# Weight part buffers at eight places of a 512-byte line, lower activations 32 bytes off the upper, in a fp32-split decoder trunk

## The chip, the core and the metric

The kernel runs on one core of one Trainium2 chip. The metric is the device time of one execution in microseconds (us); three runs of the kernel before have a median of 1153.88 us (1153.59 to 1154.02). Engines are called by the profile's names: PE (TensorE, matmuls), PEld (TensorE's weight loads), ACT (ScalarE), DVE (VectorE), POOL (GpSimd) and SP (SyncE, which here only issues DMAs).

## The reference

One decoder layer on 256 tokens of width 2048, float32 throughout:

```
h    = rms_norm(x, norm1_g)
proj = h @ w_in                       # q, k, v and forget logits of 8 heads; q, k, v of 8 more
y_a  = forgetting attention (causal softmax with cumulated log-sigmoid gates)
y_b  = mixture of three dilated windows with a relative position bias
x    = x + concat(rms_norm(y_a), rms_norm(y_b)) @ w_out
h    = rms_norm(x, norm2_g)
x    = x + square(relu(h @ w_mlp_in)) @ w_mlp_out      # 2048 -> 8192 -> 2048
out  = rms_norm(x, final_norm_g)
```

Head size is 128. Nearly all of the arithmetic is in the four weight products.

## The kernel before

**Three products for one.** A float32 operand is split into an upper part (`..._hi`, rounded to the type fp32r) and a lower part (`..._lo`, the rest), and a product is upper x upper, upper x lower and lower x upper, accumulated in PSUM. So each 128-deep slice of a weight product is three PE matmuls.

**Chunks and steps.** The weights are cut into chunks of 512 columns: twelve for q, v and k ("qkv"), eight for the output projection ("o"), and four rounds of four up chunks ("u") and four down chunks ("d"). A step is 256 rows of a chunk, two 128-deep slices. SP loads four slices by one 1 MB DMA into one of four `raw` buffers. `split` makes the parts of a step: ACT copies `raw` to `whi` with rounding (L168) and DVE subtracts to get `wlo` (L169), both 128 x 1024. There are four buffers for each (`LEAD + 1`), and `split` runs up to `LEAD` = 3 steps ahead of PE.

**Which operand lies still.** A matmul has a stationary operand, 128 x 128, brought in by a weight load of its own (PEld) while the matmul before it runs, and a moving operand that streams through. In qkv, o and d (`product`, L299 to L301) the activations are stationary and the weight part moves, 512 columns at a time. In u (`turned_product`, L313) 128 columns of a weight part are stationary and the activations `aT_hi`, `aT_lo` move, 256 columns at a time, in the order (`whi`,`aT_hi`), (`whi`,`aT_lo`), (`wlo`,`aT_hi`). The profile writes the moving operand or the stationary one first by its own rule; the shape in a matmul's row is that of the moving operand.

**Activations.** `aT_hi` and `aT_lo` hold the normed, transposed input of qkv, and later that of u. `big_hi` and `big_lo` hold the attention's output for o (named `yT`) and the squared-ReLU hidden for d (`hT`). In the last down chunk (`last_chunk`) the first four steps' weight parts are put into `aT_hi` and `aT_lo`, which are free by then, and the last four into the weight part buffers; its second half of tokens runs as two passes of 256 columns.

**Places.** Every tile has an address within its partition. In the table "place" is that address modulo 512 bytes, in the program as it was built. A 128-column float32 stationary operand is 512 bytes of a partition, and every slice that a matmul takes of these tiles starts a multiple of 512 bytes into its tile, so a tile's place is that of all its operands.

| tile | place before | place after |
|---|---|---|
| four `whi` | 160, all | 192, 320, 448, 64 |
| four `wlo` | 160, all | 256, 384, 0, 128 |
| `aT_hi` | 480 | 480 |
| `aT_lo` | 480 | 0 |
| `big_hi`, `big_lo` | 160 | 192 |
| `q`, `v` parts | 480 | 0 |
| `k` parts, `p` parts (probabilities) | 288 | 320 |
| four `raw` | 160, 288, 416, 32 | 192, 320, 448, 64 |

Before, all of these are 32 bytes past a multiple of 64; after, all but `aT_hi` are multiples of 64.

**Order.** The program's order is written out by hand (`manual_schedule`); attention work runs as `side` work between the weight products of the chunks. The causal mask for scores is `mcat`, three 128-column blocks (triangle, zeros, triangle) of the constant `pk`.

Of the kernel before, what the change touches and what calls it, by code (L numbers as in the profile page):

```python
# [11 lines left out]
F32 = mybir.dt.float32  # L12
F32R = mybir.dt.float32r
# [6 lines left out]
P = 128  # L20
D_MODEL = 2048
SEQ = 256
TB = SEQ // P
HD = 128
NH = 8
D_GRP = NH * HD
D_FF = 4 * D_MODEL
KT = D_MODEL // P
CW = 512
# [7 lines left out]
QSCALE = HD ** -0.5  # L37

LEAD = 3
WARM, WARM2 = 8, 1  # L40


def _constants():
    i = np.arange(P)
    upto = (i[:, None] <= i[None, :]).astype(np.float32)
    after = (i[:, None] > i[None, :]).astype(np.float32)
    tri = np.where(i[None, :] <= i[:, None], 0.0, NEG).astype(np.float32)
    head = (i[:, None] % 32 == np.arange(NH)[None, :]).astype(np.float32)
    pack = np.concatenate([after, -upto, tri, np.zeros((P, P), np.float32), tri, head], axis=1)

    dist = 255 - np.arange(RW)
    d = np.maximum(dist, 0)
    exact = N_BUCKETS // 2
    df = np.maximum(d.astype(np.float32), np.float32(1.0))
    large = exact + (
        np.log(df / np.float32(exact)) / np.float32(math.log(REL_MAX / exact)) * np.float32(N_BUCKETS - exact)
    ).astype(np.int32)
    bucket = np.where(d < exact, d, np.minimum(large, N_BUCKETS - 1))
    count = np.zeros(RW, np.int64)
    for window, dil in PATTERNS:  # L60
        count += (dist >= 0) & (dist % dil == 0) & (dist <= window)
    pick = np.zeros((N_BUCKETS + 1, RW), np.float32)
    pick[bucket, np.arange(RW)] = 1.0
    pick[N_BUCKETS] = np.where(count > 0, np.log(np.maximum(count, 1)), NEG)
    return np.ascontiguousarray(pack), pick
# [3 lines left out]
def kernel(  # L69
# [23 lines left out]
    one = ctx.enter_context(tc.tile_pool(name="one", bufs=1))  # L93
    two = ctx.enter_context(tc.tile_pool(name="two", bufs=2))
    wraw = ctx.enter_context(tc.tile_pool(name="wraw", bufs=4))
    wsplit = ctx.enter_context(tc.tile_pool(name="wsplit", bufs=LEAD + 1))
    psum = ctx.enter_context(tc.tile_pool(name="psum", bufs=2, space=PSUM))
    dram = ctx.enter_context(tc.tile_pool(name="dram", bufs=1, space=DRAM))
    ctx.enter_context(tc.manual_schedule())
# [30 lines left out]
    def load(i):  # L130
        if i >= len(steps) or steps[i][1] % 2 or (steps[i][0], steps[i][1] // 2) in raws:
            return
        ci, s = steps[i]
        _, _, w, r0, c0, cols, _ = chunks[ci]
        t = wraw.tile([P, 4, CW + NH], F32, name="raw")
        src = w[r0 + s * 256:r0 + s * 256 + 512, c0:c0 + cols].rearrange("(k p) c -> p k c", p=P)
        raws[ci, s // 2] = t
        if i == 0:
            return t, src
        n = 2 if i == 2 else 4  # L140
        for k in range(0, 4, n):
            nc.sync.dma_start(t[:, k:k + n, :cols], src[:, k:k + n])

    def split(i, j0=0, n=2):
        if i >= len(steps):
            return
        if j0:
            return split_rows(i, j0, n)
        ci, s = steps[i]
        t = raws[ci, s // 2][:, 2 * (s % 2):2 * (s % 2) + 2, :]  # L150
        if ci == len(chunks) - 1 and s < 4:
            hi, lo = (a[:, 4 * s:4 * s + 4, :].rearrange("p (k j) s -> p k (j s)", k=2) for a in (aT_hi, aT_lo))
        else:
            hi, lo = (wsplit.tile([P, 2, CW], F32R, name=n) for n in ("whi", "wlo"))
        if chunks[ci][5] > CW:
            f = wsplit.tile([P, 2, 2 * NH], F32R, name="wf")
            fh, fl = f[:, :, :NH], f[:, :, NH:]
            nc.gpsimd.tensor_copy(fh, t[:, :, CW:])
            nc.gpsimd.tensor_tensor(fl, t[:, :, CW:], fh.bitcast(F32), op=ALU.subtract)
            forget_w[i] = f  # L160
        splits[i] = (hi, lo)
        split_rows(i, j0, n)

    def split_rows(i, j, n):
        ci, s = steps[i]
        hi, lo = (a[:, j:j + n, :] for a in splits[i])
        t = raws[ci, s // 2][:, 2 * (s % 2) + j:2 * (s % 2) + j + n, :CW]
        nc.scalar.activation(hi, t, AF.Copy)  # L168
        nc.vector.tensor_tensor(lo, t, hi.bitcast(F32), op=ALU.subtract)  # L169
# [27 lines left out]
    fb = one.tile([P, NH], F32, name="fb")  # L197
    relx = one.tile([N_BUCKETS + 1, NH], F32, name="relx")
    nc.vector.memset(relx, 1.0)
    pk = one.tile([P, 5 * P + NH], F32, name="pk")  # L200
    pick_sb = two.tile([P, RW], F32, name="pr")[:N_BUCKETS + 1]

    def small_loads():
# [4 lines left out]
        nc.sync.dma_start(pk, pack)  # L208
        nc.sync.dma_start(pick_sb, pick)

    mcat = pk[:, 2 * P:5 * P]
    head = pk[:, 5 * P:]
    gcat = one.tile([P, TB, P], F32R, name="gcat")


# [11 lines left out]
        nc.tensor.transpose(p[:, :k1], grow[:k1], ident[:k1, :k1])  # L227
        nc.vector.tensor_copy(gT[:, k0:k1], p[:, k0:k1])

    aT_hi = one.tile([P, KT, SEQ], F32R, name="aT_hi")  # L230
    aT_lo = one.tile([P, KT, SEQ], F32R, name="aT_lo")

    def split_psum(hi, lo, src, scale=None):
# [105 lines left out]
    def at(i, f, *a):  # L339
        side.setdefault(i, []).append((f, a))  # L340
# [69 lines left out]
    relT = one.tile([P, NH, SEQ], F32, name="relT")  # L410
# [60 lines left out]
    def scores(g, h):  # L471

        half, kind = groups[g][3:]
        hd = half * 4 + h
        qh, ql = qkv[g, "q"]
        kh, kl = qkv[g, "k"]
        s = psum.tile([P, 512], F32, name="sc")
        terms = ((qh, kh), (qh, kl), (ql, kh))
        spans = ((0, 0, P), (1, P, 3 * P))
        for t, c0, c1 in spans:  # L480
            if kind == 0:
                nc.tensor.matmul(s[:, c0:c1], gate_s[:, t * P:(t + 1) * P], decay[hd][:, :c1 - c0],  # L482
                                 start=True, stop=False)
            for n, (q, k) in enumerate(terms):
                nc.tensor.matmul(  # L485
                    s[:, c0:c1], q[:, h, t * P:(t + 1) * P], k[:, h, :c1 - c0],
                    start=n == 0 and kind == 1, stop=n == 2,
                )
        decay.pop(hd, None)
        neg = two.tile([P, 3 * P], F32, name="neg")  # L490
        pr = two.tile([P, 3 * P], F32, name="pr")
        st = two.tile([P, 3, TB], F32, name="st")
        for t, c0, c1 in spans:
            add = mcat[:, c0:c1] if kind == 0 else relT[:, hd, SEQ - (c1 - c0):]
            nc.vector.tensor_tensor_reduce(  # L495
                neg[:, c0:c1], s[:, c0:c1], add, -1.0, BIG, ALU.add, ALU.min, st[:, 0, t:t + 1]
            )
        for t, c0, c1 in spans:
            nc.scalar.activation(  # L499
                pr[:, c0:c1], neg[:, c0:c1], AF.Exp, bias=st[:, 0, t:t + 1], scale=-1.0,  # L500
                accum_out=st[:, 1, t:t + 1],
            )
        nc.vector.reciprocal(st[:, 2, :], st[:, 1, :])
        for t, c0, c1 in spans:
            nc.vector.tensor_scalar(pr[:, c0:c1], pr[:, c0:c1], st[:, 2, t:t + 1], None, op0=ALU.mult)
        probs[g, h] = pr
# [134 lines left out]
    def last_chunk(done):  # L641

        ci = len(chunks) - 1
        what, key, _, _, _, _, kts = chunks[ci]
        i0 = len(steps) - kts // 2
        c0 = D_MODEL - CW
        for t, a, b, n in ((0, 0, CW, 3), (1, 0, CW // 2, 3), (1, CW // 2, CW, 4)):
            acc = psum.tile([P, CW], F32, name="acc", bufs=4)
            for kt in range(kts):
                if t == 0 and kt % 2 == 0:  # L650
                    split(done + 1 + kt // 2)
                product(acc[:, :b - a], operands(what, key), kt, t, splits[i0 + kt // 2], kt % 2, slice(a, b),
                        kt == 0, kt == kts - 1)
                if t == 0:
                    run_side(2 * i0 + kt)
            if b == CW:
                sum_before(t, n)
            add_down(acc, t, slice(c0 + a, c0 + b), n)
            if b == CW:
                finish(t, n, slice(c0 + a, c0 + b))  # L660
# [6 lines left out]
    for ci, (what, key, *_rest) in enumerate(chunks[:-1]):  # L667
# [8 lines left out]
        elif what in "qk":  # L676
# [4 lines left out]
            if what == "k":  # L681
                kind = groups[key][4]
                for h in range(4):
                    n = e + 6 + 4 * h
# [20 lines left out]

    idle_products(WARM)
    split(0, 0, 1)
    gains(0, 16)
    to_features(0, 0, 1)
    split(0, 1, 1)  # L710
    to_features(1, 0, 1)
    idle_products(WARM2)
# [13 lines left out]
    at(21, nc.vector.tensor_copy, gcat, pk[:, :2 * P].rearrange("p (t s) -> p t s", t=TB))  # L726
    ahead = 2 * LEAD + 1

    final = len(steps) - KT // 2
    upto = {final - 4: final, final - 3: final + 1, final - 2: final + 3, final - 1: final + 5}  # L730
    done = 10
    for i in range(final):
        if i:
            load(i + ahead)
        for k in range(done + 1, upto.get(i, i + LEAD) + 1):
            split(k)
            load(k + LEAD + 2)
            done = k
# [34 lines left out]
```

## Time and profile before

| | us |
|---|---|
| median of 3 runs | 1153.88 |
| the profiled execution's own time | 1154.59 |
| its span (first to last instruction) | 1152.8 |
| PE busy | 1126.7 (98%) |
| DVE busy | 638.9 (55%) |
| ACT busy | 522.0 (45%) |
| DMA, mean rate over the span | 183 GB/s |

A PE row's busy time includes the tail in which the next matmul already streams, so a group's mean is not the pace of the engine. The pace is read from the timeline: the time between the starts of two matmuls, divided by the number of matmuls between them. The granted clock is full but for short stretches at the start, between 60 and 130 us and at the end (0.989 over the span).

### The profile page before, as it was taken

To read this page: it belongs to the slowest core of one execution; us is meant where nothing else is said; L and a number is where in the kernel's file an instruction comes from. 1 tells how busy PE (TensorE), PEld (TensorE's weight loads), DVE (VectorE), ACT (ScalarE), POOL (GpSimd) and SP (SyncE) were. 2 spreads that over 40 slices of the span, in tenths; PEclk is the share of its full clock that TensorE was granted. 3 is DMA by queue.
4 is the path that set the end of the run, shared out by engine and by line. 5 is a ranking of instruction groups with operands and counts; after the bars stand their busy time and mean duration, and the time that the engine had idled before them with its cause. 6 is when DMAs were issued, how large, how long until landed. Compare 5 with 4: busy or idle time off the path is not lost.

```text
span 1152.8 us, 16038 instructions
## 1 busy us (share of the span) xinstructions
PE 1126.7 (98%) x6635; PEld 991.0 (86%) x6635; DVE 638.9 (55%) x795; ACT 522.0 (45%) x675; POOL 29.4 (3%) x56
## 2 busy tenths in 40 slices
PE   9994999999999999999999999999999999999997
PEld 6773888888888889998889998889999889999886
DVE  5652655656647665555454555544555554555564
ACT  5442544544545455444433544333444343444441
POOL 0100000000000100000000000000000000000000
PEclk9997999999999999999999999999999999999999
DMA  9666455454454455655566465566546666555641
GB/s 314 213 159 161 139 181 183 146 182 147 157 192 162 159 173 180 198 199 189 184 197 195 156 217 184 190 201 194 183 159 209 198 201 183 183 183 184 248 153 73
DMA packets 105605, 210.71 MB, mean 183 GB/s; under 512 B 3987, under 2 KB 4836, under 8 KB 105404
## 3 DMA queue, kind: packets, MB, share of 16 engines
q1 hardware_dynamic: 104556, 207.06, 55.0%
q0 software_dynamic: 976, 2.63, 1.5%
q8 instruction: 52, 0.85, 0.3%
q14 instruction: 21, 0.17, 0.0%
HBM read 206.00 MB, written 3.67 MB: 182 GB/s over the span
## 4 chain that ended last, share of the span: by engine, by line
PE 95%; issue 3%; DVE 1%; DMA 0%; POOL 0%; ACT 0%; SPq 0%; DVEq 0%; POOLq 0%; ACTq 0%
PE acc L313 31%; PE acc L299 20%; PE acc L300 20%; PE acc L301 20%; PE sc L485 1%; PE sc L530 1%; PE tr L250 1%; PE tr L455 1%; PE tr L512 0%; DMA grow<-in_norm_g_dram 0%; PE sc L333 0%; PE sc L482 0%; POOL rel_d L418 0%; ACT L380 0%; DVE wlo L169 0%
## 5 line engine op out<-in xcount | busy, mean ns | idle before, releaser
L169 DVE TENSOR_TENSOR wlo<-raw,whi 128x1024 fp32r<-128x1024 f32 (+1 forms) x381 | 463.3, 1222 | 376.8 <-ACT whi L168 374.0
L168 ACT ACTIVATE whi<-raw 128x1024 fp32r<-128x1024 f32 (+1 forms) x381 | 399.9, 1055 | 406.7 <-PE acc L300 242.9
L313 PE MATMUL acc<-aT_hi,whi 128*128 128x256 f32 x1024 | 287.3, 281 | 0.0
L313 PE MATMUL acc<-aT_lo,whi 128*128 128x256 f32 x1024 | 286.1, 279 | 0.0
L313 PE MATMUL acc<-aT_hi,wlo 128*128 128x256 f32 x1024 | 286.1, 279 | 0.0
L299 PE MATMUL acc<-whi,big_hi 128*128 128x512 f32 (+1 forms) x632 | 246.0, 389 | 0.0
L301 PE MATMUL acc<-wlo,big_hi 128*128 128x512 f32 (+1 forms) x632 | 244.7, 387 | 0.0
L300 PE MATMUL acc<-whi,big_lo 128*128 128x512 f32 (+1 forms) x632 | 244.6, 387 | 0.0
L313 PEld LDWEIGHTS acc<-aT_hi,wlo 128*128 128x128 f32 x1024 | 192.9, 188 | 0.0
L313 PEld LDWEIGHTS acc<-aT_hi,whi 128*128 128x128 f32 x1024 | 192.3, 188 | 0.2
L313 PEld LDWEIGHTS acc<-aT_lo,whi 128*128 128x128 f32 x1024 | 191.7, 187 | 0.2
L299 PE MATMUL acc<-whi,aT_hi 128*128 128x512 f32 x384 | 157.9, 411 | 0.0
L300 PE MATMUL acc<-whi,aT_lo 128*128 128x512 f32 x384 | 153.4, 400 | 0.0
L301 PE MATMUL acc<-wlo,aT_hi 128*128 128x512 f32 x384 | 153.0, 398 | 0.0
L301 PEld LDWEIGHTS acc<-wlo,big_hi 128*128 128x128 f32 x632 | 118.7, 188 | 24.5
L300 PEld LDWEIGHTS acc<-whi,big_lo 128*128 128x128 f32 x632 | 118.8, 188 | 23.2
L299 PEld LDWEIGHTS acc<-whi,big_hi 128*128 128x128 f32 x632 | 118.8, 188 | 23.1
L301 PEld LDWEIGHTS acc<-wlo,aT_hi 128*128 128x128 f32 x384 | 73.1, 190 | 17.6
L299 PEld LDWEIGHTS acc<-whi,aT_hi 128*128 128x128 f32 x384 | 73.3, 191 | 15.4 <-issue 0.6
L300 PEld LDWEIGHTS acc<-whi,aT_lo 128*128 128x128 f32 x384 | 73.4, 191 | 14.2 <-DVE aT_lo L240 0.3
L499 ACT ACTIVATE pr<-neg,st 128x128 f32<-128x128 f32 (+1 forms) x32 | 14.3, 448 | 56.2 <-DVE st L495 56.2
L237 DVE TENSOR_TENSOR big_lo<-nat,big_hi 128x512 fp32r<-128x512 f32 x32 | 22.2, 693 | 22.4 <-ACT big_hi L236 22.4
(159 smaller groups left out, 532.9 us busy)
## 6 DMA issues: line engine op xcount, KB each, us to landing
raw<-in_w_mlp_in_dram SPq DMA_DIRECT2D x64, 1024.0 KB, 5.3
raw<-in_w_mlp_out_dram SPq DMA_DIRECT2D x64, 1024.0 KB, 5.3
raw<-in_w_in_dram SPq DMA_DIRECT2D x42, 1024.0 KB, 5.2
raw<-in_w_out_dram SPq DMA_DIRECT2D x16, 1024.0 KB, 5.1
raw<-in_w_in_dram SPq DMA_DIRECT2D x4, 1040.0 KB, 5.3
raw<-in_w_in_dram SPq DMA_DIRECT2D x3, 512.0 KB, 7.5
xs<-in_x_dram SPq DMA_DIRECT2D x3, 512.0 KB, 9.0
rel_d<-neg POOLq DMA_DIRECT2D x1, 1536.0 KB, 36.6
```

The costliest lines, as they stand in the source:

```text
L168: nc.scalar.activation(hi, t, AF.Copy)
L169: nc.vector.tensor_tensor(lo, t, hi.bitcast(F32), op=ALU.subtract)
L237: nc.vector.tensor_tensor(lo, src, hi.bitcast(F32), op=ALU.subtract)
L250: nc.tensor.transpose(p[:, j * SEQ + t * P:j * SEQ + (t + 1) * P], xs[:, t, c:c + P], ident)
L299: nc.tensor.matmul(acc, xh, hi[:, j, cols], start=go, stop=False)
L300: nc.tensor.matmul(acc, xl, hi[:, j, cols], start=False, stop=False)
L301: nc.tensor.matmul(acc, xh, lo[:, j, cols], start=False, stop=end)
L313: nc.tensor.matmul(acc, w[:, j, b * P:(b + 1) * P], a[:, kt, :], start=kt == 0 and b % 2 == 0 and n == 0, stop=kt == kts - 1 and n == 2, s ...
L455: nc.tensor.transpose(p[:, j * SEQ + t * P:j * SEQ + (t + 1) * P], ts[t][:, h * P:(h + 1) * P], ident)
L485: nc.tensor.matmul(s[:, c0:c1], q[:, h, t * P:(t + 1) * P], k[:, h, :c1 - c0], start=n == 0 and kind == 1, stop=n == 2,)
L499: nc.scalar.activation(pr[:, c0:c1], neg[:, c0:c1], AF.Exp, bias=st[:, 0, t:t + 1], scale=-1.0, accum_out=st[:, 1, t:t + 1],)
L530: nc.tensor.matmul(y[:, o0:SEQ], v[:, t, h * P:(h + 1) * P], p[:, c0:c1], start=t == 0 and n == 0, stop=t == 1 and n == 2,)
```

## The change

Each of the eight weight part buffers becomes a tile of its own, 64 bytes longer than its data (`PAD` = 16 floats), so that each starts 64 bytes further in a 512-byte line than the one before it. `parts` hands them out in the same rotation as the pool did. `aT_hi` becomes 32 bytes longer, which moves `aT_lo`, and everything that is allocated behind it, by 32 bytes. The constant `pk` loses its first triangle (zeros and triangle are left, 512 bytes a partition less), and the scores take their mask from the end of what is left: the same values. On every engine the instructions, their shapes, their order and their waits stay the same; only addresses change, and the load of `pk` is 128 x 520 floats for 128 x 648.

```diff
+PAD = 16
...
-    pack = np.concatenate([after, -upto, tri, np.zeros((P, P), np.float32), tri, head], axis=1)
+    pack = np.concatenate([after, -upto, np.zeros((P, P), np.float32), tri, head], axis=1)
...
+    wpart = ctx.enter_context(tc.tile_pool(name="wpart", bufs=1))
...
+    turns = [0]
+
+    def parts():
+        n = turns[0] % (LEAD + 1)
+        turns[0] += 1
+        return [wpart.tile([P, 2 * CW + PAD], F32R, name=f"{a}{n}")[:, :2 * CW].rearrange("p (j c) -> p j c", j=2)
+                for a in ("whi", "wlo")]
...
-            hi, lo = (wsplit.tile([P, 2, CW], F32R, name=n) for n in ("whi", "wlo"))
+            hi, lo = parts()
...
-    pk = one.tile([P, 5 * P + NH], F32, name="pk")
+    pk = one.tile([P, 4 * P + NH], F32, name="pk")
...
-    mcat = pk[:, 2 * P:5 * P]
-    head = pk[:, 5 * P:]
+    mask = pk[:, 2 * P:4 * P]
+    head = pk[:, 4 * P:]
...
-    aT_hi = one.tile([P, KT, SEQ], F32R, name="aT_hi")
+    aT_hi = one.tile([P, KT * SEQ + PAD // 2], F32R, name="aT_hi")[:, :KT * SEQ].rearrange("p (k s) -> p k s", k=KT)
...
-            add = mcat[:, c0:c1] if kind == 0 else relT[:, hd, SEQ - (c1 - c0):]
+            add = mask[:, SEQ - (c1 - c0):] if kind == 0 else relT[:, hd, SEQ - (c1 - c0):]
```

## The prediction

> **What bounds the kernel.** I read the page's first and fourth parts, then the waits, then the timeline of PE stage by stage, because a change that moves nothing but addresses can only act through how long one instruction takes.
>
> ```profile
> span 1152.8 us, 16038 instructions
> PE 1126.7 (98%) x6635; PEld 991.0 (86%) x6635; DVE 638.9 (55%) x795; ACT 522.0 (45%) x675; POOL 29.4 (3%) x56
> PE 95%; issue 3%; DVE 1%; DMA 0%; POOL 0%; ACT 0%; SPq 0%; DVEq 0%; POOLq 0%; ACTq 0%
> ```
>
> ```profile
> ACT whi L168 <- PE acc L300: 242.9, 157, 2.4
> ACT whi L168 <- PE acc L313: 154.8, 97, 1.9
> PE sc L482 <- POOL gate_h L465: 15.0, 1, 15.0
> ```
>
> PE holds 95% of the chain that ended last. ACT, which makes the upper weight parts, waits nearly 400 us in all for PE to give buffers back, so weights are always there before PE needs them. PE's one long wait (15 us, for a gate tile) is not touched. So the time is the number of weight matmuls times PE's pace, and the question is whether that pace hangs on addresses.
>
> **The pace by stage.** The groups of matmuls, kept apart by shape (the number behind x is the count):
>
> ```profile
> L313 PE MATMUL acc<-aT_hi,whi 128*128 128x256 f32 x1024 | 287.3, 281 | 0.0
> L299 PE MATMUL acc<-whi,big_hi 128*128 128x512 f32 x616 | 241.5, 392 | 0.0
> L299 PE MATMUL acc<-whi,aT_hi 128*128 128x512 f32 x384 | 157.9, 411 | 0.0
> ```
>
> With the other two of each three that makes 3072 matmuls in u, 1848 in o and d that move a weight part 512 wide, and 1152 in qkv. Their means already differ between o and d (392 ns) and qkv (411 ns), though shape, type and engine are the same. The starts tell it better. First d: 180 matmuls lie between these two.
>
> ```profile
> 524.13 0.39 PE L301 MATMUL acc<-wlo,big_hi 128*128 128x512 f32 x1
> ...
> 564.96 0.39 PE L301 MATMUL acc<-wlo,big_hi 128*128 128x512 f32 x1
> ```
>
> 40.83 / 180 = 226.8 ns. In qkv 124 lie between the next two, with nothing else on PE in between:
>
> ```profile
> 154.66 0.40 PE L300 MATMUL acc<-whi,aT_lo 128*128 128x512 f32 x1
> ...
> 183.59 0.39 PE L301 MATMUL acc<-wlo,aT_hi 128*128 128x512 f32 x1
> ```
>
> 28.93 / 124 = 233.3 ns. For u the chain of waits has one unbroken piece:
>
> ```profile
> 610.91 90.45 PE acc L313 x768
> ```
>
> 90.45 / 768 = 117.8 ns.
>
> **Is it the place?** qkv and d differ in what is stationary (`aT` at place 480, `big` at 160) but also in what else runs. The last down chunk is cleaner: same stationary tile, same shape, one stretch behind the other, and only the moving tile changes from `aT` (480) to the weight parts (160).
>
> ```profile
> 1121.58 0.40 PE L299 MATMUL acc<-aT_hi,big_hi 128*128 128x512 f32 x1
> ...
> 1127.09 0.40 PE L299 MATMUL acc<-whi,big_hi 128*128 128x512 f32 x1
> ...
> 1132.58 0.28 PE L299 MATMUL acc<-aT_hi,big_hi 128*128 128x256 f32 x1
> ...
> 1135.41 0.29 PE L299 MATMUL acc<-whi,big_hi 128*128 128x256 f32 x1
> ...
> 1136.01 0.28 PE L301 MATMUL acc<-wlo,big_hi 128*128 128x256 f32 x1
> ...
> 1138.17 0.28 PE L301 MATMUL acc<-wlo,big_hi 128*128 128x256 f32 x1
> ```
>
> 512 wide from `aT`: 24 starts in 5.51 us, 229.6 ns, against d's 226.8. 256 wide from `aT`: 24 in 2.83 us, 117.9 ns, u's own pace to 0.1 ns; 256 wide from the weight parts: 18 in 2.16 us, 120.0 ns. The pace follows the pair of tiles, to a fraction of a nanosecond, and not the stage. I take it that the places (address modulo 512) are what differs; the trace cannot exclude another part of the address.
>
> The Trainium skill, page "SBUF — State Buffer", section "Who interferes with whom", says "PE and ACT never wait on anyone." By that sentence the pace could not hang on where tiles lie and the sum would be 0 us; the rows above disagree with it, as far as PE's two own streams go.
>
> **The extra per matmul.** 256 more columns cost 226.8 - 120.0 = 106.8 ns at the same places, so the bare streaming is about 213.5 ns for 512 and 106.7 for 256. What lies above it, by pair of places (moving, stationary):
>
> - (160, 160), d: 13.4 ns at 512 and 13.3 at 256
> - (480, 160): 16.2 at 512; 11.1 at 256, in u and in the last chunk
> - (160, 480), qkv: 19.9
> - (288, 480), the attention's value products at 256 wide: three starts in the next rows, 0.34 / 3 = 113.3 ns, so 6.6
>
> ```profile
> 153.75 0.28 PE L530 MATMUL sc<-p_hi,v_hi 128*128 128x256 f32 x1
> 153.86 0.28 PE L530 MATMUL sc<-p_lo,v_hi 128*128 128x256 f32 x1
> 153.97 0.28 PE L530 MATMUL sc<-p_hi,v_lo 128*128 128x256 f32 x1
> 154.09 0.22 PE L530 MATMUL sc<-p_hi,v_hi 128*128 128x128 f32 x1
> ```
>
> **The change part by part.**
>
> *Weight parts at eight places, moving (qkv, o, d).* After, each of three pairs is replaced by eight, evenly spread: `big` at 192, `aT_hi` at 480 and `aT_lo` at 0 against 192, 256, ... 128. No row shows these pairs. The bounds are the lowest and highest extra seen, 6.6 and 19.9 ns. Between ends that far apart I take the mean of the four pairs seen, (13.4 + 16.2 + 19.9 + 6.6) / 4 = 14.0, because spreading over a whole line is what makes a mean. o and d: (14.0 - 13.4) x 1848 = +1.1 us, between -12.6 and +12.0. qkv: (14.0 - 19.9) x 1152 = -6.8 us, between -15.3 and 0. qkv sits on the worst pair seen, and d on the best of those at 512; spreading gives qkv much and costs d little.
>
> *Weight parts stationary, `aT_hi` still moving from 480 (two of three in u, 2048 matmuls).* 0 us, since u and the last chunk have the same 256-wide pace. Both had their stationary tile at 160, so the bounds stay 6.6 and 13.3: -9.2 to +4.5 us.
>
> *`aT_lo` 32 bytes on, moving from 0 (one of three in u, 1024).* Mean of the 256-wide extras (13.3 + 11.1 + 6.6) / 3 = 10.3 for 11.1: -0.8 us, bounds -4.6 to +2.3.
>
> *ACT's and DVE's places, and the DMAs'.* `raw` goes through four places even before, and ACT's split ranges very little over them, as DVE's does:
>
> ```profile
> L168 ACT ACTIVATE whi<-raw x381: 621/1060/1066, 5.0 to 1125.6; 128x1024 fp32r<-128x1024 f32 x190, 128x512 fp32r<-128x512 f32 x1
> L169 DVE TENSOR_TENSOR wlo<-raw,whi x381: 693/1226/1235, 5.6 to 1126.9; 128x1024 fp32r<-128x1024 f32 x190, 128x512 fp32r<-128x512 f32 x1
> ```
>
> Median and maximum lie within 1%, while ACT waits for PE nearly as long as it works. 0 us. If PE got 3% faster, 35 us, that cover of some 400 us would still be there.
>
> *The mask and its load.* Sixteen DVE additions (0.29 to 0.42 us) read the same shape at another address, and the one load of `pk`, issued at 21.3 us and first read at 47.0, is a fifth smaller: 0 us, hidden behind PE's weight products.
>
> ```profile
> L495 DVE CUSTOM_DVE_ANT_0 neg<-sc,pk x16: 291/355/421, 112.7 to 212.5; 128x128 f32<-128x128 f32 x8, 128x256 f32<-128x256 f32 x8
> L208 SPq DMA_DIRECT2D pk<-in_pack_dram x1: 417/417/417, 21.3 to 21.3; - x1
> L665 DVE CAST gcat<-pk x1: 284/284/284, 47.0 to 47.0; 128x256 fp32r<-128x256 f32 x1
> ```
>
> Sum: +1.1 - 6.8 - 0.8 = -6.5 us. Against the profiled execution's 1154.59 us (1.8 us of it outside the span, unchanged) that is 1148.1; the median of the runs is 0.7 us lower, so 1147.4.
>
> **Rivals.**
>
> *The start on a multiple of 64 is what counts (large gain).* Before, every operand started 32 bytes past one; after, only `aT_hi` does. If a stream that starts so loses a fixed piece, the weight parts and `aT_lo` drop to the lowest extra seen: -6.8 x 1848 - 13.3 x 1152 - 4.5 x 1024 = -12.6 - 15.3 - 4.6 = -32.5 us, 1121. For it: no row before shows an aligned weight stream, so the room is there. Against it: the extra of unaligned streams already varies from 6.6 to 19.9, so 32 bytes past 64 is not the whole of it.
>
> The Trainium skill, page "TensorE: Matmul & The Clock Gate", section "Back-to-back issue gap", gives N/2.4 + 2.5 ns, 215.8 at 512 columns and 109.2 at 256. By it the whole room is an estimated 67 us, which would end at 1087; no row here comes down to it at these widths.
>
> *d loses its favourable pair (slower).* Moving and stationary operand at one place is the best 512-wide pair in the trace, and some three fifths of the time in `product` is spent with it (1848 x 226.8 ns against 1152 x 233.3). If the seven other distances cost what the two others seen do, (16.2 + 19.9) / 2 = 18.1 ns, o and d pay +4.7 x 1848 = +8.7 us, qkv gains only 1.8 x 1152 = 2.1, and u, with its stationary places scattered, goes half way to 13.3: +1.1 x 3072 = +3.4. Sum +10 us, 1164. It decides as soon as the mean extra in o and d is above 13.4 + 7.6 / 1848 us = 17.5 ns while the rest goes as forecast. Against it stands only the 6.6 ns of the value products.
>
> *Nothing.* The pace hangs on something else of the address (which of the large tiles), or gains and losses cancel: 1153.9.
>
> **Chances.** Spreading to the mean, -2.3 to -15 us: 0.40, own range 1139 to 1151. Large gain by alignment: 0.22. Slower: 0.24. Within 0.2% (2.3 us, about what this measurement can tell from no change): 0.14. So faster 0.62, same 0.14, slower 0.24. The range 1121 to 1163 reaches to the centres of the two outer cases; I leave 0.1 beyond each end.
>
> **What would show it.** Right: qkv's pace falls from 233.3 to about 227.5, d's is no longer one number but changes from step to step with the buffer in turn, mean about 227.4; u's stays near 117.8 with `aT_lo`'s matmuls different from the others. Alignment: qkv and d both fall to about 220 in every step. Slower: d's mean above 231. What would make the whole wrong is a pace that does not change by step in d although the eight places do: then place modulo 512 is not the variable. ACT, DVE and DMA rows should not move.

## The result: slower by 0.8%, the wrong way

The changed kernel takes 1162.14 us (median of 4 runs, 1161.36 to 1165.64) against 1153.74 us for the kernel before in the same session. The ratio is 1.008, with a 95% interval of 1.0059 to 1.0101. Forecast was 1147.4 us: the sign was wrong, and the time is near that of the rival "d loses its favourable pair", 1164.

The page after, first and fourth part. PE is as full as before, with 8 us more in the same 6635 matmuls (1126.7 us before):

```profile
span 1159.6 us, 16038 instructions
PE 1134.9 (98%) x6635; PEld 991.9 (86%) x6635; DVE 639.9 (55%) x795; ACT 522.1 (45%) x675; POOL 29.1 (3%) x56
PE 94%; issue 3%; DVE 1%; DMA 1%; ACT 0%; POOL 0%; SPq 0%; DVEq 0%; POOLq 0%; ACTq 0%
```

The groups by shape. L311 to L313 are L299 to L301 of before, L325 is L313; between the bars stand the busy time in us and the mean of one matmul in ns:

```profile
L325 PE MATMUL acc<-aT_hi,wlo 128*128 128x256 f32 x1024 | 289.6, 283 | 0.0
L325 PE MATMUL acc<-aT_lo,whi 128*128 128x256 f32 x1024 | 287.9, 281 | 0.0
L325 PE MATMUL acc<-aT_hi,whi 128*128 128x256 f32 x1024 | 286.6, 280 | 0.0
L311 PE MATMUL acc<-whi,big_hi 128*128 128x512 f32 x616 | 243.8, 396 | 0.0
```

A weight part moving against `big` was 392 ns and is 396. In u the three matmuls of a group had 281, 279 and 279 before and have 280, 281 and 283 now. The timeline gives the paces. In d, 48 matmuls (four steps, each buffer once) lie between these two starts:

```profile
779.54 0.39 PE L311 MATMUL acc<-whi,big_hi 128*128 128x512 f32 x1
...
790.65 0.28 PE L325 MATMUL acc<-aT_hi,whi 128*128 128x256 f32 x1
```

11.11 us / 48 = 231.5 ns, for 226.8. In qkv 125 lie between the next two, 29.09 / 125 = 232.7 (before 233.3 over 124):

```profile
151.48 0.45 PE L311 MATMUL acc<-whi,aT_hi 128*128 128x512 f32 x1
...
180.57 0.39 PE L313 MATMUL acc<-wlo,aT_hi 128*128 128x512 f32 x1
```

And u's unbroken piece in the chain of waits: 91.09 / 768 = 118.6 ns, for 117.8.

```profile
610.87 91.09 PE acc L325 x768
```

Over all steps without other work between, the timeline's means are 231.4 for 226.8 in o and d, 232.4 for 233.3 in qkv and 118.6 for 117.8 in u. Times the counts: +4.6 x 1848 = +8.5 us, -0.9 x 1152 = -1.0 and +0.8 x 3072 = +2.5, sum +10.0. The runs show +8.4. The two profiled executions differ by 6.8. In the one after, PE's wait for the gate tile was 1.3 us shorter (13.7 for 15.0), and of the stretch behind it, in which the granted clock is 0.50 and 512-wide matmuls start 427 ns apart, 4 such matmuls were left for 11. Why the medians differ by less than the paces was not followed further.

What the forecast put at nothing for ACT held: its split goes from 621/1060/1066 ns (least, median, most) to 621/1060/1068, and ACT still waits for PE:

```profile
L180 ACT ACTIVATE whi<-raw x381: 621/1060/1068, 4.5 to 1132.3; 128x1024 fp32r<-128x1024 f32 x190, 128x512 fp32r<-128x512 f32 x1
```

```profile
ACT whi L180 <- PE acc L312: 248.2, 161, 2.2
ACT whi L180 <- PE acc L325: 156.7, 97, 1.9
```

One thing in the timeline pointed to the cause. In d the gaps between starts change from matmul to matmul, as foreseen, but buffers 0 and 2 have the same sequence of gaps, to 1 ns, and so have 1 and 3. Those buffers are 256 bytes apart, modulo 512. That suggests that what counts is the place modulo 256, so that there were only four different places, not eight.

### The profile page after: what moved, and what is told of

It is laid out like the page before. It is cut to its first block, busy times and chain, and to the rows that moved or that the text cites. A ratio compares the mean times of both kernels' runs of the same rounds, so it can differ in the third digit from the quotient of the medians.

```text
span 1159.6 us, 16038 instructions
## 1 busy us (share of the span) xinstructions
PE 1134.9 (98%) x6635; PEld 991.9 (86%) x6635; DVE 639.9 (55%) x795; ACT 522.1 (45%) x675; POOL 29.1 (3%) x56
## 4 chain that ended last, share of the span: by engine, by line
PE 94%; issue 3%; DVE 1%; DMA 1%; ACT 0%; POOL 0%; SPq 0%; DVEq 0%; POOLq 0%; ACTq 0%
PE acc L325 31%; PE acc L311 20%; PE acc L312 20%; PE acc L313 20%; PE sc L497 1%; PE sc L542 1%; DMA raw<-in_w_in_dram 1%; PE tr L262 1%; PE tr L467 1%; PE tr L524 0%; PE sc L345 0%; DVE wlo L181 0%; PE sc L494 0%; ACT whi L180 0%; POOL rel_d L430 0%
## 5 line engine op out<-in xcount | busy, mean ns | idle before, releaser
L325 PE MATMUL acc<-aT_hi,wlo 128*128 128x256 f32 x1024 | 289.6, 283 | 0.0
L325 PE MATMUL acc<-aT_lo,whi 128*128 128x256 f32 x1024 | 287.9, 281 | 0.0
L325 PE MATMUL acc<-aT_hi,whi 128*128 128x256 f32 x1024 | 286.6, 280 | 0.0
L311 PE MATMUL acc<-whi,big_hi 128*128 128x512 f32 (+1 forms) x632 | 248.3, 393 | 0.0
L313 PE MATMUL acc<-wlo,big_hi 128*128 128x512 f32 (+1 forms) x632 | 246.5, 390 | 0.0
L325 PEld LDWEIGHTS acc<-aT_hi,whi 128*128 128x128 f32 x1024 | 193.3, 189 | 0.2
L325 PEld LDWEIGHTS acc<-aT_hi,wlo 128*128 128x128 f32 x1024 | 193.0, 188 | 0.0
L325 PEld LDWEIGHTS acc<-aT_lo,whi 128*128 128x128 f32 x1024 | 192.3, 188 | 0.2
L311 PE MATMUL acc<-whi,aT_hi 128*128 128x512 f32 x384 | 156.6, 408 | 0.0
L313 PE MATMUL acc<-wlo,aT_hi 128*128 128x512 f32 x384 | 151.9, 396 | 0.0
L313 PEld LDWEIGHTS acc<-wlo,big_hi 128*128 128x128 f32 x632 | 118.6, 188 | 27.3
L312 PEld LDWEIGHTS acc<-whi,big_lo 128*128 128x128 f32 x632 | 118.7, 188 | 25.6
L311 PEld LDWEIGHTS acc<-whi,big_hi 128*128 128x128 f32 x632 | 118.7, 188 | 25.6
L313 PEld LDWEIGHTS acc<-wlo,aT_hi 128*128 128x128 f32 x384 | 72.6, 189 | 16.9
L311 PEld LDWEIGHTS acc<-whi,aT_hi 128*128 128x128 f32 x384 | 72.7, 189 | 15.3 <-ACT fu L392 0.6
```

Source lines behind the costliest of these rows:

```text
L311: nc.tensor.matmul(acc, xh, hi[:, j, cols], start=go, stop=False)
L312: nc.tensor.matmul(acc, xl, hi[:, j, cols], start=False, stop=False)
L313: nc.tensor.matmul(acc, xh, lo[:, j, cols], start=False, stop=end)
L325: nc.tensor.matmul(acc, w[:, j, b * P:(b + 1) * P], a[:, kt, :], start=kt == 0 and b % 2 == 0 and n == 0, stop=kt == kts - 1 and n == 2, s ...
```

## The experiments

Theory A: the pace is set by the distance from the place of the moving operand to that of the stationary one, modulo 256, and by nothing else of the address. Theory B: it is the change from one place to another between neighbouring matmuls that costs. Theory C: what counts is whether a stream starts on a multiple of 64 bytes, as in the prediction's first rival. All kernels below keep the shortened mask; they only move tiles. The edits are shown against the changed kernel or, where the text says so, against the experiment before.

**The map: four distances in one kernel.** Both parts of a buffer share a place, and the buffers step by 64 bytes, so each step of 12 (or 24) matmuls has one distance and time to settle.

```diff
-        return [wpart.tile([P, 2 * CW + PAD], ...)[:, :2 * CW]... for a in ("whi", "wlo")]
+        hi = wpart.tile([P, 2 * CW], F32R, name=f"whi{n}")
+        lo = wpart.tile([P, 2 * CW + PAD], F32R, name=f"wlo{n}")[:, :2 * CW]
...
-    aT_hi = one.tile([P, KT * SEQ + PAD // 2], ...)
+    aT_hi = one.tile([P, KT, SEQ], F32R, name="aT_hi")
```

> Upper and lower part of a buffer share one place; the four buffers stand 0, 64, 128 and 192 bytes beyond the place of big (160); aT stays at 480 for both parts. Theory A (distance: the pace is set by the distance between moving and stationary operand, modulo 256, since in the changed kernel the buffers 256 bytes apart have the same pace): the four buffers have four paces, d in buffer 0 at 226.7 ns as before and dearer in the others, qkv in buffer 1 (distance 0 from aT) also at 226.7, u in buffer 0 at 117.8 and in buffer 1 at 120.0. Theory B (change of place: only the step of the moving operand from one place to another between neighbouring matmuls costs): d at 226.7 to 227.2 in every buffer, qkv at 233.3 in every buffer, total within 2 us of 1154. Theory C (start on a multiple of 64): all starts are 32 past one as before, so all paces as before.

1161.98 us (one run). The timeline of d, at the seventh matmul and at the end of the steps of buffers 0, 1, 2 and 3 (six matmuls between the rows of a pair):

```profile
782.02 0.39 PE L312 MATMUL acc<-whi,big_hi 128*128 128x512 f32 x1
...
783.38 0.40 PE L312 MATMUL acc<-whi,big_hi 128*128 128x512 f32 x1
...
784.77 0.39 PE L312 MATMUL acc<-whi,big_hi 128*128 128x512 f32 x1
...
786.14 0.40 PE L312 MATMUL acc<-whi,big_hi 128*128 128x512 f32 x1
...
787.54 0.39 PE L312 MATMUL acc<-whi,big_hi 128*128 128x512 f32 x1
...
788.94 0.39 PE L312 MATMUL acc<-whi,big_hi 128*128 128x512 f32 x1
...
790.34 0.39 PE L312 MATMUL acc<-whi,big_hi 128*128 128x512 f32 x1
...
791.74 0.28 PE L326 MATMUL acc<-aT_hi,whi 128*128 128x256 f32 x1
```

1.36, 1.37, 1.40 and 1.40 us for six: about 226.7, 228.9, 233.1 and 233.3 ns (means over some 30 steps each, without one step of buffer 0 and two of buffer 2 that had not settled). Four buffers, four paces, so B alone falls, which wanted 226.7 in all. In qkv the same buffers have other distances, because `aT` lies elsewhere. Buffer 1 is now the one at distance 0 (256 modulo 512):

```profile
161.87 0.39 PE L312 MATMUL acc<-whi,aT_hi 128*128 128x512 f32 x1
...
163.23 0.40 PE L312 MATMUL acc<-whi,aT_hi 128*128 128x512 f32 x1
```

1.36 / 6 = 226.7 ns, where qkv's settled steps had 233.3 before (eight of ten such steps have 226.7; two had not settled). That settles the modulus too: 256 bytes apart counts as together.

**The same, 32 bytes further** (against the first map).

```diff
+        g = PAD // 2 if n == 0 else 0
-        hi = wpart.tile([P, 2 * CW], F32R, name=f"whi{n}")
+        hi = wpart.tile([P, g + 2 * CW], F32R, name=f"whi{n}")[:, g:]
```

> As the kernel with the buffers at 0, 64, 128, 192 bytes beyond big, but all four 32 bytes further: 32, 96, 160 and 224 beyond it, and so each weight part starts on a multiple of 64 while big and aT start 32 past one. Theory A: four paces again, none of them 226.7 in d, since no distance is 0. Theory B: 226.7 in d and 233.3 in qkv in every buffer. Theory C: d and qkv at about 220 in every buffer, and u as before.

1170.68 us (one run), the slowest kernel here. Buffer 0 in d, where the weight parts start on multiples of 64:

```profile
788.90 0.40 PE L313 MATMUL acc<-whi,big_hi 128*128 128x512 f32 x1
...
790.30 0.40 PE L313 MATMUL acc<-whi,big_hi 128*128 128x512 f32 x1
```

1.40 / 6 = 233.3; the other three are the same to 0.6 ns. Theory C, which had about 220, is out: aligning the weight stream gives nothing.

**Finer steps** (against the first map). `big` 16 bytes and `aT` 8 bytes into their (longer) tiles, buffers as in the first map.

```diff
-    aT_hi = one.tile([P, KT, SEQ], F32R, name="aT_hi")
+    aT_hi = one.tile([P, KT * SEQ + 64], F32R, name="aT_hi")[:, 2:2 + KT * SEQ].rearrange("p (k s) -> p k s", k=KT)
...
-    yT_hi = one.tile([P, 2 * NH, SEQ], F32R, name="big_hi")
+    yT_hi = one.tile([P, KT * SEQ + 64], F32R, name="big_hi")[:, 4:4 + KT * SEQ].rearrange("p (k s) -> p k s", k=KT)
```

> Buffers at 0, 64, 128, 192 bytes beyond 160 as in the first map, big 16 bytes further (distances 16, 208, 144, 80) and aT 8 bytes further (in qkv 72, 8, 200, 136). Theory A says that the pace depends on the distance and not in which step: if finely, distance 8 and 16 lie between 226.7 (at 0) and 233.3 (at 32); if the line is read in pieces of 32 bytes, 8 and 16 have the pace of 0 or of 32. Theory B: nothing changes against the first map.

1168.83 us (one run). Buffer 0 in d (distance 16) and buffer 1 in qkv (distance 8), six matmuls each:

```profile
786.12 0.39 PE L312 MATMUL acc<-whi,big_hi 128*128 128x512 f32 x1
...
787.48 0.39 PE L312 MATMUL acc<-whi,big_hi 128*128 128x512 f32 x1
```

```profile
163.24 0.39 PE L312 MATMUL acc<-whi,aT_hi 128*128 128x512 f32 x1
...
164.62 0.39 PE L312 MATMUL acc<-whi,aT_hi 128*128 128x512 f32 x1
```

Neither branch of the expectation held alone: distance 16 settles at 226.7 like 0 (in 26 of 31 steps), distance 8 gives 230.5. Nor is the price smooth between the coarser steps: 231.8 at 80, for 233.3 and 233.9 at 64 and 96, and 231.1 at 200 and 231.7 at 208. In u the four finer distances give 118.7 to 120.5. At 512 columns each of the finer distances was seen in one stage only.

The three maps together, settled pace in ns by distance (stationary less moving, modulo 256), from the second half of all undisturbed steps (at 0, and in d at 128, the one or two steps that had not settled are left out; with them 0 has 226.8 and 227.4):

| distance | 0 | 32 | 64 | 96 | 128 | 160 | 192 | 224 |
|---|---|---|---|---|---|---|---|---|
| 512 wide, d (`big` stationary) | 226.7 | 233.4 | 233.3 | 233.9 | 233.1 | 233.3 | 228.9 | 233.5 |
| 512 wide, qkv (`aT` stationary) | 226.7 | 233.3 | 233.3 | 234.1 | 232.7 | 233.3 | 228.8 | 233.4 |
| 256 wide, u (`aT` moving) | 119.8 | 118.3 | 118.0 | 118.8 | 118.7 | 119.8 | 117.6 | 117.0 |

The first two rows come from different tiles at different addresses, in different stages, and agree within 0.4 ns. That is the strongest evidence for Theory A where the distance stays the same through a step. At 512 wide, 0 and 192 are cheap, and the six other multiples of 32 cost about 6.5 ns more than 0.

**One part alone: the weight parts.**

```diff
-    aT_hi = one.tile([P, KT * SEQ + PAD // 2], F32R, name="aT_hi")[:, :KT * SEQ].rearrange("p (k s) -> p k s", k=KT)
+    aT_hi = one.tile([P, KT, SEQ], F32R, name="aT_hi")
```

> Only the eight places of the weight parts; aT_lo is not moved, so everything but the weight parts lies at its old place (modulo 512). Theory A and B: o and d have the same distances and the same changes of place as in the changed kernel, so the same 231.4 ns, +8.5 us; qkv within 1.5 ns of 233; u dearer by about 0.8 ns, +2.5 us; in all 1160 to 1166. Theory C: as the weight parts then start 32 past a multiple of 64 again, the loss would come from there, and the time is 1154 or above 1166.

1161.93 us, ratio 1.0069 (1.0052 to 1.0085). Its group of L311 against `big` is the changed kernel's:

```profile
L311 PE MATMUL acc<-whi,big_hi 128*128 128x512 f32 x616 | 244.0, 396 | 0.0
```

d runs at 231.4, qkv at 232.9, and u at 118.0, where 118.6 was expected. The weight parts start 32 past a multiple of 64 again, so the loss comes from this part, and not from alignment; u's further 0.6 ns in the changed kernel needs both parts.

**The other part alone: the lower activations.**

```diff
-        return [wpart.tile([P, 2 * CW + PAD], F32R, ...
+        return [wpart.tile([P, 2 * CW], F32R, ...
```

> Only the 32 bytes behind aT_hi; all eight weight parts share one place (192), that of big, on a multiple of 64. Theory A and B: d at 226.7, since distance and constancy of place are as before; qkv changes only where aT_hi is stationary (distance 32 for 64); in all 1150 to 1156. Theory C: all operands but aT_hi start on a multiple of 64: d at about 220, in all about 1135.

1151.83 us, ratio 0.9982 (0.9973 to 0.9991): a small gain. Every operand of d starts on a multiple of 64 here, and 48 matmuls take 10.88 us, 226.7 ns, as before:

```profile
775.01 0.39 PE L311 MATMUL acc<-whi,big_hi 128*128 128x512 f32 x1
...
785.89 0.28 PE L325 MATMUL acc<-aT_hi,whi 128*128 128x256 f32 x1
```

The gain is qkv's, 231.2 for 233.3 (-2.5 us by the pace, -2.0 measured in all). There the distances take turns between 32 and 64. Each alone has 233.3 in the map, and together they have 2.1 less: so a mixture isn't the mean of its parts, and here it is cheaper, where Theory B had each change cost.

**Two distances taking turns.** All buffers alike, lower parts 64 bytes beyond upper ones, so that d has distances 0, 0, 192.

```diff
+        hi = wpart.tile([P, 2 * CW + PAD], F32R, name=f"whi{n}")[:, :2 * CW]
+        lo = wpart.tile([P, 2 * CW + 3 * PAD], F32R, name=f"wlo{n}")[:, :2 * CW]
```

> All four upper parts at the place of big (160), all four lower parts 64 bytes beyond it; aT as before the change. So every step of d has the distances 0, 0 and 192 (stationary less moving, modulo 256) that the changed kernel has in its buffers 0 and 2. Theory A alone (each matmul has the pace of its own distance): (2 x 226.7 + 228.9) / 3 = 227.4 ns in d. Theory A with B on top (two distances taking turns cost by themselves): 231 to 232 ns in d in every step, as in the changed kernel's buffers 0 and 2.

1162.54 us (one run). Between these 48 matmuls lie 11.13 us, 231.9 ns (232.0 over all steps):

```profile
781.55 0.39 PE L312 MATMUL acc<-whi,big_hi 128*128 128x512 f32 x1
...
792.68 0.28 PE L326 MATMUL acc<-aT_hi,whi 128*128 128x256 f32 x1
```

The mean of its own distances would be 227.4. So taking turns costs 4.6 ns here, with the same in every buffer. In qkv the same kernel mixes the distances 64, 64 and 0: the mean by the map would be 231.1, and the timeline has 234.3, dearer than either alone. A holds for steady distances; where distances take turns the map gives no price, and what a mixture costs has to be measured.

**Everything at one place.** The weight parts lose their padding, and `aT` starts 192 bytes into a 256-byte longer tile, so that all of it lies at 160 modulo 256 like `big` and the weight parts. u gets names of its own for its activations, still at the same place.

```diff
+    aT = [one.tile([P, KT * SEQ + 64], F32R, name=n) for n in ("aT_hi", "aT_lo")]
+    (aT_hi, aT_lo), (uT_hi, uT_lo) = ([a[:, o:o + KT * SEQ].rearrange("p (k s) -> p k s", k=KT) for a in aT] for o in (48, 48))
...
-        terms = ((hi, aT_hi), (hi, aT_lo), (lo, aT_hi))
+        terms = ((hi, uT_hi), (hi, uT_lo), (lo, uT_hi))
```

> All weight parts, big and aT at one place (160), nothing spread. Theory A: qkv falls from 233.3 to 226.7 (-6.7 ns x 1152 = -7.7 us), u rises from 117.8 to 120.0 (+2.2 x 3072 = +6.8 us), o and d as before; in all 1151 to 1154. Rival (spreading as such is what helped qkv in the changed kernel and hurt d): no change of qkv, 1154.

1156.34 us, ratio 1.0019 (1.0010 to 1.0028). qkv has 48 matmuls in 10.90 us, 227.1 with the unsettled start of the first step in it, and u 92.15 / 768 = 120.0 ns:

```profile
233.83 0.40 PE L313 MATMUL acc<-whi,aT_hi 128*128 128x512 f32 x1
...
244.73 0.39 PE L313 MATMUL acc<-whi,aT_hi 128*128 128x512 f32 x1
```

```profile
608.66 92.15 PE acc L327 x768
```

Both paces are as Theory A had them, and the rival (spreading as such helps qkv) falls: qkv gains more without any spreading. The time is 2 us above the expected range; the same two waits as in the next kernel are there (15.7 us for the gate tile, 2.7 at the start).

**A place for each use** (against the kernel with everything at one place). qkv reads its activations from place 160 (distance 0 from the weight parts); u's activations are written 32 bytes further into the same buffer (distance 224).

```diff
-    ... for a in aT] for o in (48, 48))
+    ... for a in aT] for o in (48, 56))
```

> Weight parts and big at one place (160); qkv takes its activations from the same place (distance 0), u takes its own from 32 bytes further in the same buffer (distance 224, the cheapest at 256 columns in the map). Theory A: qkv 226.7 (-7.7 us), u 117.0 (-0.8 x 3072 = -2.5 us), o and d 226.7: 1143 to 1146. Rival: 1154.

1146.52 us, ratio 0.9931 to the kernel before (0.9919 to 0.9944): faster than both kernels, and half a microsecond outside the expected 1143 to 1146. u's piece is 89.60 / 768 = 116.7 ns, and qkv's 48 matmuls take 10.90 us:

```profile
606.23 89.60 PE acc L327 x768
```

```profile
233.91 0.40 PE L313 MATMUL acc<-whi,aT_hi 128*128 128x512 f32 x1
...
244.81 0.39 PE L313 MATMUL acc<-whi,aT_hi 128*128 128x512 f32 x1
```

By the paces it should have gained 6.3 x 1152 = 7.3 us in qkv (227.0 for 233.3 over all steps) and 1.1 x 3072 = 3.4 in u. The timeline gives u and d together 3.5 us less, but the first o matmul starts only 3.8 us earlier (330.0 for 333.8). PE's waits show where part of that went (the profiled execution, 1147.28 us, is the slowest of the five):

```profile
PE sc L496 <- POOL gate_h L479: 15.4, 1, 15.4
PE tr L263 <- DVE aT_lo L253: 2.3, 1, 2.3
```

The wait for the gate tile ends behind a DMA of POOL's (`rel_d`, 36.3 us from issue to landing, 36.6 before), and so what PE gains between that issue and the wait is waited away. And the start, where the first weights arrive, cost a wait of 2.3 us that the profile before does not have. Whether that one comes from the layout or from the execution is open: it is 2.3 to 2.9 us in four of the kernels here, 1.7 with the weight parts alone, 0.5 in the changed kernel and not there with the lower activations alone.

## Why the prediction was wrong

*What bounds the kernel, and that the pace hangs on the pair of places:* right. PE's paces alone add up to the change and 1.6 us more; ACT's rows did not move, and the kernel with the shortened mask and the lower activations alone is not slower than the kernel before.

*The variable:* half right. It is the distance between the two operands that stream together, but modulo 256, not 512. With 512 I counted eight places where there were four.

*The step that failed* is the first of the part by part, "I take the mean of the four pairs seen, 14.0, because spreading over a whole line is what makes a mean". It was given +1.1 us in o and d and -6.8 in qkv, and they measured +8.5 and -1.0. Two things were wrong in it. First, the value it rested on: 6.6 ns for the attention's value products pulled the mean down. Their distance is 192, and in long runs at 256 columns the map has 117.6 ns there, an extra of 10.9; the 6.6 came out of one burst of three matmuls between others, which is not a settled pace (that the burst is the reason is argued, not shown; over all 16 heads these starts average 115.0 ns, so the burst that was taken was a low one besides). Without it the mean of the other three is 16.5, by which d would lose 5.7 us and qkv gain 3.9: that alone turns the forecast into about no change. The measured extra in o and d is 231.4 - 213.4 = 18.0. Second, the distances are not spread evenly in price: at 512 columns one is best, one near it, and six cost the same 233. d already had the best one, so spreading could only lose there; qkv had one of the six, and met mostly others of the six.

*How far the map accounts for it.* In the changed kernel d has the distances 0, 0, 192 in buffers 0 and 2 and 128, 128, 64 in buffers 1 and 3. Their own prices have the mean 230.3 ns, 3.5 above 226.8, and 231.4 was measured: about three quarters of the loss is the price of the places, and the rest is what taking turns adds. That rest has two signs: buffers 0 and 2 run at 231.7, 4.3 above the mean of their distances, and buffers 1 and 3 at 231.0, 2.1 below theirs. In qkv the prices have the mean 232.7, and 232.4 was measured.

*The rival that came near.* "d loses its favourable pair" had 18.1 ns, +8.7 us in o and d and 1164 us; 18.0, +8.5 and 1162.1 were measured. Its sign rests on the right reason, that d had the best of the 512-wide pairs seen. That its size fits so well is in part luck: it had seven of eight distances at 18.1, where a third of d's matmuls kept distance 0 and a sixth the cheap 192, and mixing made up the difference.

*u:* the term "0 us, since u and the last chunk have the same 256-wide pace" rested on a place of `aT_hi` that was seen against one stationary place only, and with `aT_lo` u was given -0.8. It measured +2.5 us for all of u; the map ranges from 117.0 to 119.8 by distance.

*One reading:* the 229.6 ns of the last chunk, held against d's 226.8, has the unsettled starts of a stretch in it; the stretch behind it in the same rows, at the places of d, has 5.49 / 24 = 228.8 ns. The stretch from `aT` has distance 192, and the map has 228.9 there, so its extra of 16.2 should be 15.5. That changes little.

*Alignment* was given 0.22; no kernel here shows an effect of it (d has 226.7 ns at distance 0 with all operands on a multiple of 64 and with all 32 past one).

The Trainium skill, page "TensorE: Matmul & The Clock Gate", section "Step-by-step: what each phase is for", says that loading the next tile's weights does not steal read bandwidth from the running matmul. No run here measures bandwidth. What the runs show is that the pace still hangs on the two tiles together: at equal shapes it goes from 226.7 to 234.1 ns by the place of the stationary tile against the one that streams.

## What to carry to other kernels

When PE is the bound and two kinds of matmul with the same shape have different paces, look at where their operands lie. With the fp32r operands of this kernel, the only type measured, the same offset modulo 256 bytes was best where 512 columns move, and at 256 columns the moving operand 32 bytes beyond the stationary one; other widths and types have to be measured. Keep one distance through a stretch, because the price of a mixture can't be told from its parts. Before averaging over unknown cases, ask whether the present one is the best of them; spreading a layout trades the good case for the others. And take a pace from long settled runs, not from bursts of three.

## What the runs showed that was not expected

A matmul with 512 fp32r columns takes 226.7 ns when the stationary tile lies 0 or 16 bytes beyond the moving one modulo 256, 228.9 at 192 and 233 to 234 at 32, 64, 96, 128, 160 and 224. Steps with the same distance repeat this within about 0.5 ns in most cases; at 0 and 16 some steps had not settled by their second half. With 256 columns it is 116.7 at 224 when all of u has that distance, and 120.0 at 0. Distances that take turns do not average: 0, 0, 192 gave 232.0, 64, 64, 0 gave 234.3, and 32 with 64 gave 231.2. What in the chip makes these numbers is open: no experiment here went below the distance. In steps with one distance the stationary tile in use and the one being loaded behind it lie at the same place, so these runs do not tell which of the two counts against the moving one.
